# Scaling tokens by expert weights: one weight load in 1 KB runs with block transposes, a first tile in two pieces, and a 512-byte store by each DMA engine

## The chip, the cores and the metric

The kernel runs on one core of a Trainium2 chip. The metric is the device time of one execution in microseconds. Data lies in the chip's HBM; a kernel brings it into the on-chip memory (SBUF, 128 partitions) by DMA, computes there, and stores it by DMA. The core has 16 DMA engines, which serve the queues of all issuing engines. Two engines issue DMAs here: SyncE (SP), through the queue that the profile calls q1, and ScalarE (ACT), through q10. The two compute engines at work are VectorE (DVE) and ScalarE.

## The reference

```python
batch, seq, hidden, k = 16, 1024, 512, 2
x_expanded = x[:, :, np.newaxis, :].repeat(k, axis=2)
weights = expert_weights[..., np.newaxis]
return (x_expanded * weights).astype(np.float32)
```

Each of the 16384 tokens is a row of 512 float32 values. The output has two rows per token: the row times its first weight, and the row times its second. The expert indices are not used. The input is 33.6 MB, the output 67.1 MB, the weights 131 KB.

## The kernel before

The tokens are cut into eight groups of 2048. In a group, partition p holds 16 consecutive tokens (`TX = 16`), so that a group's input is one tile of 128 partitions by 8192 floats, 32 KB in one run for each partition (4 MB in all). `rows` (line 46) makes this view for input, output and weights alike. Input tiles come from `x_pool`, which has two buffers. A group is computed in two halves of eight tokens (`TO = 8`); each half fills one output tile of 128 by 8192 floats (4 MB) from `o_pool`, which has four buffers.

The weights are loaded first, by eight DMAs issued by SP (line 55), one for each group: 128 partitions by 32 floats, which is a run of 128 bytes for each partition. All end up in one tile `w_tile`, where column c of partition p is the weight that belongs to slot c of that partition's tokens.

`load(i)` (lines 69 to 77) takes an input buffer and issues the group's load from ScalarE (line 76). Two loads are issued ahead of the loop; after each group the load of the group after next follows. A load can be issued when both compute engines are through with the tile that had its buffer. In ScalarE's program it stands behind the first multiply of the next group.

The loop over a group's 16 tokens issues two multiplies for each: for `kk == 0` a `tensor_scalar` on VectorE (line 97), for `kk == 1` a `mul` on ScalarE (line 91). Each reads 512 columns of the input tile and one column of `w_tile`, and writes 512 columns of the output tile. After eight tokens SP issues the store of the output tile (line 105). SP and ScalarE work their programs in order: an instruction that waits holds up those behind it.

Of the kernel before, what the change touches and what calls it, by code (L numbers as in the profile page):

```python
# [1 line left out]

# [4 lines left out]


@with_exitstack
def kernel(  # L10
    ctx: ExitStack,
    tc: tile.TileContext,
    x: bass.AP,
    expert_indices: bass.AP,
    expert_weights: bass.AP,
    out: bass.AP,
):
    nc = tc.nc

    batch, seq, hidden = x.shape  # L20
    k = expert_weights.shape[-1]
    P = nc.NUM_PARTITIONS
    ntok = batch * seq
    assert ntok % P == 0
    A_TOTAL = ntok // P

    f32 = mybir.dt.float32
    row = k * hidden
    TX = 16
    TO = 8  # L30


    groups = [[16], [16], [16], [16], [16], [16], [16], [16]]
    assert sum(sum(g) for g in groups) == A_TOTAL

    xf = x.rearrange("b s h -> (b s) h")
    of = out.rearrange("b s k h -> (b s) (k h)")
    wf = expert_weights.rearrange("b s k -> (b s) k")

    w_pool = ctx.enter_context(tc.tile_pool(name="w_pool", bufs=1))  # L40
    x_pool = ctx.enter_context(tc.tile_pool(name="x_pool", bufs=2))
    o_pool = ctx.enter_context(tc.tile_pool(name="o_pool", bufs=4))

    w_tile = w_pool.tile([P, A_TOTAL * k], f32)

    def rows(of_all, done, T):
        return of_all[done * P : (done + T) * P, :].rearrange(
            "(p a) n -> p (a n)", a=T
        )

    weights = []
    for group in groups:
        weights.append((sum(n for _, n in weights), sum(group)))
    for at, T in weights:
        nc.sync.dma_start(out=w_tile[:, at * k : (at + T) * k], in_=rows(wf, at, T))

    tiles = []
    done = 0
    for group in groups:
        T = sum(group)  # L60
        a0 = 0
        for n in group:
            tiles.append((done, T, a0, n))
            a0 += n
        done += T

    loaded = []

    def load(i):
        if i >= len(tiles):  # L70
            return
        done, T, a0, n = tiles[i]
        x_tile = x_pool.tile([P, TX * hidden], f32)
        cols = rows(xf, done, T)[:, a0 * hidden : (a0 + n) * hidden]
        for lo, hi in [(0, P)]:
            nc.scalar.dma_start(out=x_tile[lo:hi, : n * hidden], in_=cols[lo:hi, :])  # L76
        loaded.append(x_tile)

    for i in range(2):
        load(i)  # L80
    for i, (done, T, a0, n) in enumerate(tiles):
        x_tile = loaded[i]
        outr = rows(of, done, T)
        for t in range(n):
            if t % TO == 0:
                o_tile = o_pool.tile([P, TO * row], f32)
            for kk in range(k):
                c = (done + a0 + t) * k + kk
                o = t % TO * row + kk * hidden
                if kk == 1:  # L90
                    nc.scalar.mul(  # L91
                        out=o_tile[:, o : o + hidden],
                        in_=x_tile[:, t * hidden : (t + 1) * hidden],
                        mul=w_tile[:, c : c + 1],
                    )
                    continue
                nc.vector.tensor_scalar(  # L97
                    out=o_tile[:, o : o + hidden],
                    in0=x_tile[:, t * hidden : (t + 1) * hidden],
                    scalar1=w_tile[:, c : c + 1],  # L100
                    scalar2=None,
                    op0=mybir.AluOpType.mult,
                )
            if (t + 1) % TO == 0:
                nc.sync.dma_start(
                    out=outr[:, (a0 + t + 1 - TO) * row : (a0 + t + 1) * row],
                    in_=o_tile,
                )
        load(i + 2)

# [1 line left out]
_INS = ['x', 'expert_indices', 'expert_weights']  # L112
_OUTS = [((16, 1024, 2, 512), 'float32')]


# [23 lines left out]
```

## Time and profile before

| | |
|---|---|
| median of 12 runs | 240.16 us (240.04 to 241.89) |
| the profiled execution | 240.13 us |
| its span, first to last instruction | 238.3 us |
| VectorE busy | 52.0 us, 128 multiplies of 483 ns |
| ScalarE busy | 81.4 us, 128 multiplies of 711 ns and a table load of 1.28 us |
| DMA packets on SP's queue | 3456, 67.24 MB |
| DMA packets on ScalarE's queue | 1152, 33.55 MB |
| HBM read, written | 33.69 MB, 67.11 MB |

The span is what the trace covers; 1.8 us of the measured time lie around it. A DMA is carried out as packets, one for each run of memory[...], with one packet of 4 bytes at the end that counts the DMA's semaphore. A large load or store is thus 128 packets of 32 KB, eight for each engine. The "DMA" row of the page gives the mean busy share of the 16 engines in tenths, for 40 slices of the span; the row "GB/s" gives what they moved, where the bytes of a packet count in the slice in which it starts. An instruction that issues a DMA ends long before the data lands: the landing has its own figure.

### The profile page before, as it was taken

What the parts mean: (1) busy time and instruction counts of PE and PEld (TensorE: products, weight loads), DVE (VectorE), ACT (ScalarE), POOL (GpSimd) and SP (SyncE); (2) the same over time, 40 slices, a digit from 0 to 9 for tenths busy, and PEclk for the clock granted to TensorE, in tenths of its full rate; (3) what the DMA queues carried; (4) which work ended last, traced back from release to release, by engine and by line L of the source; (5) the groups of instructions that cost most, each with busy time, mean ns of one, the idle gap of its engine ahead of it and who ended that gap; (6) DMA issues with size and microseconds to landing.
All of it is one profiled execution on the core that took longest, in us unless ns stands there. A gap on an engine that the chain in (4) does not pass through costs nothing.

```text
span 238.3 us, 384 instructions
## 1 busy us (share of the span) xinstructions
DVE 52.0 (22%) x128; ACT 81.4 (34%) x129; POOL 0.2 (0%) x4
## 2 busy tenths in 40 slices
DVE  0072900055005004050230503214040235000000
ACT  2078960076107007080260803417043256200000
POOL 0000000000000000000000000000000000000000
DMA  6999999999999999999999999999999999999996
GB/s 267 442 442 362 435 434 429 418 429 418 434 440 440 432 440 440 434 429 434 423 429 429 429 434 440 440 434 434 440 429 429 440 423 429 429 429 434 440 440 264
DMA packets 4610, 100.81 MB, mean 423 GB/s; under 512 B 1536, under 2 KB 1536, under 8 KB 1536
## 3 DMA queue, kind: packets, MB, share of 16 engines
q1 hardware_dynamic: 3456, 67.24, 65.6%
q10 hardware_dynamic: 1152, 33.55, 33.1%
q14 instruction: 2, 0.02, 0.0%
HBM read 33.69 MB, written 67.11 MB: 423 GB/s over the span
## 4 chain that ended last, share of the span: by engine, by line
DMA 60%; another core or an unknown queue 12%; ACT 12%; ACTq 1%; issue 0%
DMA out_dram<-o_tile 41%; DMA x_tile<-in_x_dram 18%; ACT o_tile L91 12%; DMA w_tile<-in_expert_weights_dram 1%; ACTq L76 0%; ACTq L134 0%; ACTq L91 0%
## 5 line engine op out<-in xcount | busy, mean ns | idle before, releaser
L91 ACT ACTIVATE o_tile<-x_tile,w_tile 128x512 f32<-128x512 f32 x128 | 80.2, 711 | 118.6 <-DMA out_dram<-o_tile 96.1
L97 DVE TENSOR_SCALAR o_tile<-x_tile,w_tile 128x512 f32<-128x512 f32 x128 | 52.0, 483 | 150.2 <-DMA out_dram<-o_tile 115.7
L91 ACT ACT_TABLE_LOAD x1 | 1.3, 1283 | 3.8 <-DMA w_tile<-in_expert_weights_dram 3.8
L123 POOL MEMSET const-bfloat16-1.0<- 128x1 bf16 x1 | 0.1, 103 | 0.0
L123 POOL MEMSET const-uint8-127<- 128x1 uint8 x1 | 0.1, 102 | 0.0
L123 POOL MEMSET const-float32-0.0<- 128x1 f32 x1 | 0.1, 100 | 0.2 <-issue 0.2
L123 POOL MEMSET const-float32-1.0<- 128x1 f32 x1 | 0.1, 99 | 0.0
## 6 DMA issues: line engine op xcount, KB each, us to landing
out_dram<-o_tile SPq DMA_DIRECT2D x16, 4096.0 KB, 48.3
x_tile<-in_x_dram ACTq DMA_DIRECT2D x8, 4096.0 KB, 23.2
w_tile<-in_expert_weights_dram SPq DMA_DIRECT2D x8, 16.0 KB, 21.1
```

The lines of the kernel that those rows point to most:

```text
L91: nc.scalar.mul(out=o_tile[:, o : o + hidden], in_=x_tile[:, t * hidden : (t + 1) * hidden], mul=w_tile[:, c : c + 1],)
L97: nc.vector.tensor_scalar(out=o_tile[:, o : o + hidden], in0=x_tile[:, t * hidden : (t + 1) * hidden], scalar1=w_tile[:, c : c + 1], scala ...
L123: nc = _bacc.Bacc("TRN2", target_bir_lowering=False, num_devices=1)
```

## The change

The eight weight loads become one DMA, issued by ScalarE ahead of all input: the weights are read as 128 runs of 256 floats (1 KB) into `w_in`. They then lie in the wrong partitions. One VectorE transpose of 128 by 256 turns each 32 by 32 block, into `w_mid`, and 16 transposes of 32 partitions by 64 elements move and turn the blocks into their places in `w_tile`. The layout of `w_tile` is that of before.

SP issues one additional store ahead of all else: a tile `early` of 16 partitions by 128 floats, which VectorE sets to zero, goes to the first 512 bytes of 16 output rows, 128 rows apart, one row for each DMA engine. The real stores write these rows later.

The first group's input is loaded by two DMAs, each of eight tokens for every partition (16 KB runs). ScalarE has one small multiply on the loaded weights (`unused`) ahead of the loop. The multiplies are given out by `c % 3`: every third goes to ScalarE, the others to VectorE (171 and 85, for 128 and 128). The number and size of the output tiles, the stores and the seven other input loads are as before.

```diff
-    weights = []
-    for group in groups:
-        weights.append((sum(n for _, n in weights), sum(group)))
-    for at, T in weights:
-        nc.sync.dma_start(out=w_tile[:, at * k : (at + T) * k], in_=rows(wf, at, T))
+    w_in = w_pool.tile([P, R * C], f32)
+    w_mid = w_pool.tile([P, R * C], f32)
+    w_tile = w_pool.tile([P, G * C], f32)
+    nc.scalar.dma_start(out=w_in, in_=wf.rearrange("(p n) -> p n", p=P))
+    early = w_pool.tile([16, 128], f32)
+    nc.vector.memset(early, 0.0)
+    nc.sync.dma_start(
+        out=of[: P * TX, :128].rearrange("(e t) n -> e t n", e=16)[:, 0, :], in_=early
+    )
...
-        for lo, hi in [(0, P)]:
-            nc.scalar.dma_start(out=x_tile[lo:hi, : n * hidden], in_=cols[lo:hi, :])
+        at = 0
+        for n in [8, 8] if i == 0 else [TX]:
+            cols = slice(at * hidden, (at + n) * hidden)
+            nc.scalar.dma_start(out=x_tile[:, cols], in_=rows(xf, i)[:, cols])
+            at += n
...
+    nc.vector.transpose(out=w_mid, in_=w_in)
+    GQ = G // (P // B)
+    for dst in range(P // B):
+        for src in range(P // B):
+            nc.vector.transpose(
+                out=w_tile[
+                    dst * B : (dst + 1) * B, src * GQ * C : (src + 1) * GQ * C
+                ],
+                in_=w_mid[src * B : (src + 1) * B, :].rearrange(
+                    "c (q g h j) -> c g h j q", q=R, g=GQ, h=P // B
+                )[:, :, dst],
+            )
+    unused = w_pool.tile([P, 1], f32)
+    nc.scalar.mul(out=unused, in_=w_in[:, :1], mul=w_in[:, :1])
...
-                c = (done + a0 + t) * k + kk
+                c = i * C + t * k + kk
...
-                if kk == 1:
+                if c % 3 == 2:
```

Here `P` is 128, `B` is 32, `TX` is 16, `k` is 2, `C` is 32, `R` and `G` are 8.

More of the change, by code (lines that the diff above doesn't have):

```diff
@@ L30 @@
     TO = 8
-    groups = [[16], [16], [16], [16], [16], [16], [16], [16]]
-    assert sum(sum(g) for g in groups) == A_TOTAL
+    G = A_TOTAL // TX
+    C = TX * k
+    B = 32
+    R = 8
+    assert A_TOTAL % TX == 0 and C == B and G * (P // B) == B and A_TOTAL * k == R * B
     xf = x.rearrange("b s h -> (b s) h")
     of = out.rearrange("b s k h -> (b s) (k h)")
-    wf = expert_weights.rearrange("b s k -> (b s) k")
+    wf = expert_weights.rearrange("b s k -> (b s k)")
     w_pool = ctx.enter_context(tc.tile_pool(name="w_pool", bufs=1))
@@ L42, with rows @@
     o_pool = ctx.enter_context(tc.tile_pool(name="o_pool", bufs=4))
[L44 to L48, printed above, removed]
-        )
-    weights = []
-    for group in groups:
-        weights.append((sum(n for _, n in weights), sum(group)))
-    for at, T in weights:
[L55 to L65, printed above, removed]
+    def rows(of_all, g):
+        return of_all[g * P * TX : (g + 1) * P * TX, :].rearrange(
+            "(p a) n -> p (a n)", a=TX
+        )
+    w_in = w_pool.tile([P, R * C], f32)
[7 more added lines that the diff above has]
+    )
     loaded = []
     def load(i):
-        if i >= len(tiles):
+        if i >= G:
             return
-        done, T, a0, n = tiles[i]
         x_tile = x_pool.tile([P, TX * hidden], f32)
-        cols = rows(xf, done, T)[:, a0 * hidden : (a0 + n) * hidden]
-        for lo, hi in [(0, P)]:
-            nc.scalar.dma_start(out=x_tile[lo:hi, : n * hidden], in_=cols[lo:hi, :])
+        at = 0
[3 more added lines that the diff above has]
+            at += n
         loaded.append(x_tile)
@@ L80 @@
         load(i)
-    for i, (done, T, a0, n) in enumerate(tiles):
+    nc.vector.transpose(out=w_mid, in_=w_in)
[12 more added lines that the diff above has]
+    nc.scalar.mul(out=unused, in_=w_in[:, :1], mul=w_in[:, :1])
+    for i in range(G):
         x_tile = loaded[i]
-        outr = rows(of, done, T)
-        for t in range(n):
+        for t in range(TX):
             if t % TO == 0:
@@ L95 @@
                     )
[L96 to L103, printed above, removed]
+                else:
+                    nc.vector.tensor_scalar(
+                        out=o_tile[:, o : o + hidden],
+                        in0=x_tile[:, t * hidden : (t + 1) * hidden],
+                        scalar1=w_tile[:, c : c + 1],
+                        scalar2=None,
+                        op0=mybir.AluOpType.mult,
+                    )
             if (t + 1) % TO == 0:
                 nc.sync.dma_start(
-                    out=outr[:, (a0 + t + 1 - TO) * row : (a0 + t + 1) * row],
+                    out=rows(of, i)[:, (t + 1 - TO) * row : (t + 1) * row],
                     in_=o_tile,
```

## The prediction

> **What bounds the kernel now.** I read the page's 40 slices first, then the span cut into stretches, then the single microseconds of the worst stretch, then the waits, and last the DMA packets. From the page:
>
> ```profile
> DMA  6999999999999999999999999999999999999996
> GB/s 267 442 442 362 435 434 429 418 429 418 434 440 440 432 440 440 434 429 434 423 429 429 429 434 440 440 434 434 440 429 429 440 423 429 429 429 434 440 440 264
> ...
> DMA packets 4610, 100.81 MB, mean 423 GB/s; under 512 B 1536, under 2 KB 1536, under 8 KB 1536
> ```
>
> The 16 DMA engines are busy from the first slice to the last, while VectorE has 52.0 us of work and ScalarE 81.4 us in 238.3. What is to be seen is where the rate falls below its level: in the first slice, the fourth and the last. The stretches give the sizes (columns: stretch and length, busy time of the engines, clock, DMA share, GB/s):
>
> ```profile
> 0.00:1.00 1.00, 0.00 (x0) 0.00 (x0) 0.20 (x4) 1.00 0.00 0
> 1.00:4.00 3.00, 0.00 (x0) 0.23 (x1) 0.00 (x0) 1.00 0.84 300
> 4.00:20.00 16.00, 6.43 (x16) 7.86 (x13) 0.00 (x0) 1.00 1.02 436
> 20.00:24.00 4.00, 0.13 (x1) 3.25 (x7) 0.00 (x0) 1.00 0.99 293
> 24.00:48.00 24.00, 6.87 (x18) 10.46 (x17) 0.00 (x0) 1.00 1.01 434
> 48.00:204.00 156.00, 38.53 (x95) 59.66 (x96) 0.00 (x0) 1.00 1.00 433
> 204.00:236.00 32.00, 0.00 (x0) 0.00 (x0) 0.00 (x0) 1.00 1.00 432
> 236.00:238.30 2.30, 0.00 (x0) 0.00 (x0) 0.00 (x0) 1.00 0.00 0
> ```
>
> Loads with stores (24 to 204) and stores alone (204 to 236) run at the same 432 to 434, so the middle and the end have nothing to give. 100.81 MB at 433 are 232.8 us. What is not streaming: 1.00 us before any packet; 3 x (1 - 300/433) = 0.92 in 1 to 4, where the first loads start up; 4 x (1 - 293/433) = 1.29 in 20 to 24; 2.3 at the end. Only the front can change. Inside the bad stretch (bytes count at a packet's start):
>
> ```profile
> 20.00:21.00 1.00, 0.00 (x0) 1.00 (x3) 0.00 (x0) 1.00 0.87 230
> 21.00:22.00 1.00, 0.00 (x0) 1.00 (x3) 0.00 (x0) 1.00 1.26 329
> 22.00:23.00 1.00, 0.00 (x0) 1.00 (x2) 0.00 (x0) 1.00 0.07 10
> 23.00:24.00 1.00, 0.13 (x1) 0.25 (x2) 0.00 (x0) 1.00 1.76 603
> ```
>
> The packet records say what happens. A 32 KB packet takes 1.213 us and follows the one before it on its engine after 1.209. The last 16 packets of the second load (from 20.7) take 1.81 to 2.37, mean 2.04: a **stall of 0.83 us** on every engine. Then 0.46 (1.29 - 0.83) goes until the first store's packets start at 23.3 to 23.9, and in it the engines work off a **backlog of weight packets**. The store had been issued at 18.24, but stood behind them on SP's queue:
>
> ```profile
> 0.73 12.79 SPq L55 DMA_DIRECT2D w_tile<-in_expert_weights_dram  x8
> 18.24 6.41 SPq L105 DMA_DIRECT2D out_dram<-o_tile  x2
> ...
> DMA to landing us min/median/max: 2.7/21.1/22.4
> ```
>
> The last line is for the weights: 16 KB take 21 us to land. The cause: from 6 to 20 us each engine takes one weight packet (13 ns) per 32 KB input packet.
>
> **A rule against the row.** The Trainium skill (DMA: Bandwidth & Descriptors, Queues, rings and completion order) has an engine drain a packet of 9 to 17 descriptors before it turns to the other queue. By that, the 64 weight descriptors of an engine would be through after some 5 input packets (64/13), no backlog would meet the store, and removing the weights would save only their own time. The records show one for one, so I go by the row: the backlog's 0.46 is real, and goes. By the rule my sum is 0.46 smaller.
>
> **The change part by part.**
>
> Weights: eight loads of 128 B runs (1024 packets) become one of 128 runs of 1 KB, ahead of the input on ScalarE's queue. Removed: the backlog, 0.46. Also the interleaving: an input packet with a weight packet before it starts 1.219 us after the last, not 1.209, for some 14 packets per engine: 0.14. Added at the front: 131 KB at 433 are 0.30, less the first weight load that stood there already (9 packets of about 11 ns, 0.10): +0.20. Issue order: the first input DMA is now second on ScalarE, and an issue there took 0.41. Bounds 0 to 0.41; before, the first input packets waited for a weight packet's end on each engine anyway (starts from 1.81 to 3.02), so I take 0.10.
>
> First tile in two pieces: 16 packets of 16 KB per engine for 8 of 32 KB, plus a semaphore packet, at some 10 ns each (the extra that a small packet cost above): bounds 0 to 0.10, taken 0.06. It brings the first computation forward. The first tile landed at 13.20; half its bytes are 4.84 us less, plus 0.36 for the additions: about 8.7. This is hidden, as is the next part.
>
> Transposes: 17 on VectorE, after the weights land (first weight load: 2.7 us after issue; here about 3.6). None is in the trace. The nearest row is the multiply of 512 elements, 483 ns, 396 start to start. Upper end: 16 x 0.40 + 0.48 = 6.9, done at 10.5. The Trainium skill (VectorE: DVE Perf Modes, The TRN2 errata) prices an SBUF operation at 58 cycles plus its elements: (58 + 64)/0.96 = 127 ns, so 16 x 0.127 + 0.33 = 2.4, done at 6.0. I take the middle, 8.3. Either way the first store can be issued between 13.1 and 14.9, against 18.24. The cover is the second load, whose packets last until about 22: between 6 and 8 us of slack (to 20.9, see the last rival).
>
> Split of the multiplies: every third one goes to ScalarE, so a half tile is 10 to 11 on VectorE (x 0.396 = 4.35) and 5 to 6 on ScalarE (x 0.612 = 3.4), against 5.01 for ScalarE's 8. Hidden behind 9.7 us of store per half tile; worth nothing. If compute set the pace, VectorE's 171 x 0.396 = 68 us in 238 would still be far from it.
>
> Small store: 16 x 512 B on SP, after a VectorE memset (about 0.1). Behind it on SP are only the real stores, the first due at 13; that one overwrites the same rows and so waits for this one's landing, long past. ScalarE's dummy multiply waits for the weights with only its table load and the multiplies behind it. Direct cost: a 512 B packet, about 0.03. **The unknown** is the 0.83 stall. It falls where each engine first has a store to this output ahead of it. If it is the price of a first store, the small store pays it at 2 to 3 us, when each engine's first packet is slow anyway (1.2 to 1.95 us). Bounds: it overlaps fully (0) or is added there (0.83). Taken 0.10, since both delays would be waits and not work.
>
> A second rule speaks against this part: the same DMA page gives each DMA a fixed cost of about 2.0 us (Anatomy of one DMA) and says to coalesce transfers under 64 KB (Rules for kernel authors). Read as time on the path, the 8 KB store and the extra piece are +4.0 and the time is over 242. The row: the first 16 KB weight load took 2.65 from issue to landing, yet input packets started from 1.81 on the same engines. It is latency beside other work; I do not charge it.
>
> Sum: -0.83 - 0.46 - 0.14 + 0.20 + 0.10 + 0.06 + 0.10 + 0.03 = -0.94. The profiled execution took 240.13 (span 238.3 and 1.8 around it), the median is 240.16, so nothing shifts between them: **239.2**.
>
> **Does anything starve later?** First store from about 14, alternating one for one with the second load: both end near 33. The second store (ready at 18) then has 9.7 us to run; the third load is issued when tile 1 arrives (33.5, behind ScalarE's first multiply of it, as before), and the third store is ready at about 38. SP's queue never empties, so from there it is the old steady state, paced by stores giving back buffers:
>
> ```profile
> DVE o_tile L97 <- DMA out_dram<-o_tile: 115.7, 11, 13.8
> ACT o_tile L91 <- DMA out_dram<-o_tile: 96.1, 11, 12.0
> ```
>
> Compute waits for stores, not stores for compute.
>
> **Rivals.**
>
> Stall stays: the 0.83 belongs to the first large store, or to any turn from loads to stores, or the small store adds it at the front. For it: the first 32 KB stores themselves are not slow, so the tie to a first store is a guess. Against: one for one at 6 to 20 us, reads of weights stalled nothing. Sum -0.94 + 0.83 = -0.1: 240.0. No measurable change.
>
> More is gained: ScalarE's weight load and the small store also absorb the slow start of the first input packets (0.6 at least of the 0.92 in 1 to 4): 239.2 - 0.7 = 238.5.
>
> Slower: the transposes bring the weights late. Reading with a stride, one might cost far more than the multiply. It decides when the first store is issued later than about 20.9, as the second load's packets end at 22 and an issue took 1.0 to its first packet. Less 4.35 of compute and 3.6 for the weights, 13.0 is left for 17: 0.76 us each. At 1 us each, 4 us more of idle DMA: 243.2. Against it: twice the longest VectorE instruction in the trace. The latency rule above would land on the same side.
>
> **Numbers.** Forecast 239.2: 0.56. More gained: 0.10. Stall stays: 0.25. Slower: 0.09. A measurement of this kernel tells 0.3% (0.7 us) from no change: faster is below 239.44, slower above 240.88. The forecast's own range is 238.7 to 239.7: issue order up to 0.31 dearer or 0.10 cheaper, a late disturbance of single engines (at 77.9 us two packets were 0.4 and 0.7 late) there or not, and a part of the first packets' slow start gained; about a tenth of it is past 239.44. Faster 0.62, same 0.29, slower 0.09. To hold 8 in 10 the range takes in both neighbours: 238.3 to 240.2.
>
> **What would show it.** Right: the fourth slice near 430; no packets over 1.3 us around the end of the second load; packets under 512 B near 430; first store issued between 13 and 15. The small store's part: first input packets not ending later than 4.4 us. Stall stays: packets near 2 us wherever the first large store begins. Wrong: idle DMA after 20 us, or a first store later than 20.9.

## The result

The changed kernel takes 241.83 us (median of 12 runs, 240.74 to 244.31), against 240.19 before (49 runs measured along with it, 240.01 to 242.05). The ratio is 1.0071, with a 95% interval of 1.0048 to 1.0093: slower by 1.6 us. The profiled execution took 241.28, with a span of 239.5, and is among the faster half of the 12; the one before took 240.13, with 238.3. The ratios here compare means and leave disturbed runs out (of these 12 the one of 244.31), so they need not equal the ratio of the two medians.

The page of the changed kernel, the row of busy DMA engines, the rate and the packets:

```profile
DMA  7999999999999999999999999999999999999995
GB/s 248 432 394 438 438 432 428 438 389 427 432 432 438 438 432 438 427 439 438 438 432 427 432 421 432 438 421 432 438 432 438 421 434 438 427 438 438 432 432 219
DMA packets 3779, 100.83 MB, mean 421 GB/s; under 512 B 432, under 2 KB 576, under 8 KB 576
```

The hole in the fourth slice (362 before) is gone, and the packets under 512 B went from 1536 to 432. These 432 are the 4-byte semaphore packets alone, one from each of the 16 engines for each of 27 DMAs; before, there were 512 of them and the 1024 of the weights. But there are new holes: 394 in the third slice and 389 in the ninth. In stretches of 3 us (columns as in the prediction: stretch, length, busy time of VectorE, ScalarE and GpSimd, clock, DMA share, GB/s):

```profile
12.00:15.00 3.00, 2.67 (x7) 1.55 (x3) 0.00 (x0) 1.00 1.02 437
15.00:18.00 3.00, 2.89 (x8) 1.63 (x3) 0.00 (x0) 1.00 1.04 350
18.00:21.00 3.00, 0.00 (x0) 0.00 (x0) 0.00 (x0) 1.00 1.12 470
46.00:49.00 3.00, 0.00 (x0) 0.00 (x0) 0.00 (x0) 1.00 1.14 492
49.00:52.00 3.00, 0.00 (x0) 0.00 (x0) 0.00 (x0) 1.00 0.98 350
```

The kernel before, two of the same stretches:

```profile
15.00:18.00 3.00, 3.00 (x9) 3.00 (x6) 0.00 (x0) 1.00 0.97 416
49.00:52.00 3.00, 1.69 (x5) 3.00 (x6) 0.00 (x0) 1.00 0.94 404
```

In both holes of the changed kernel the DMA engines are busy (shares of 1.04 and 0.98) while little is begun: their packets take longer. The packet records name them. From 15.0 to 18.4 it is the third to fifth packets of the second load, right after the first store was issued at 13.20. From 49.7 to 50.6 it is nearly always the seventh of the third load, 0.39 to 0.64 us late on each engine.

I followed the packets of each DMA engine (one starts where the one before it on that engine ended) and took the mean over the 16 engines. "Excess" is what a packet takes above the usual time of its size. 192 packets of 1.213 us, or as many bytes in smaller ones, are 232.9 us in both kernels. The rest:

| us, mean of the 16 engines | before | changed |
|---|---|---|
| start of the first input packet | 2.33 | 2.61 |
| excess of packets over their usual time, start to 8 us | 0.39 | 0.59 |
| the same, 8 to 26 us (first store) | 0.84 | 0.82 |
| the same, after 26 us | 0.11 | 0.80 |
| gaps less overlaps between packets, to 26 us | +0.54 | -0.08 |
| the same, after 26 us | -0.46 | -0.43 |
| mean end of an engine's work | 236.7 | 237.2 |
| end of the last engine's work | 237.20 | 238.13 |

The weights' backlog is gone, as predicted (0.54 to -0.08). The stall at the first store has stayed (0.84, 0.82). The start is 0.5 dearer. Read stalls, which are load packets that take longer than usual, have come in the middle of the run (0.80, against 0.11), where nothing was expected; some executions of the kernel before have them too, as a later section shows. And the last engine ends 0.9 after the mean, against 0.55: the time is that of the slowest engine, not of the mean. Of the 1.15 us between the two profiles 0.55 are the mean engine's, 0.4 the last engine's distance from it, and 0.2 come after the last packet.

### The profile page after: what moved, and what is told of

It is laid out like the page before. It is cut to its first block, busy times and chain, and to the rows that moved or that the text cites. A ratio compares the mean times of both kernels' runs of the same rounds, so it can differ in the third digit from the quotient of the medians.

```text
span 239.5 us, 397 instructions
## 1 busy us (share of the span) xinstructions
DVE 73.9 (31%) x189; ACT 55.2 (23%) x87; POOL 0.2 (0%) x4
## 4 chain that ended last, share of the span: by engine, by line
DMA 72%; DVE 7%; another core or an unknown queue 5%; ACTq 1%; issue 0%; DVEq 0%; ACT 0%; SPq 0%
DMA out_dram<-o_tile 40%; DMA x_tile<-in_x_dram 32%; DVE o_tile L118 7%; ACTq L79 0%; DVEq L155 0%; ACTq L60 0%; DVEq L118 0%; ACT o_tile L112 0%; SPq L126 0%; ACTq L112 0%
## 5 line engine op out<-in xcount | busy, mean ns | idle before, releaser
L118 DVE TENSOR_SCALAR o_tile<-x_tile,w_tile 128x512 f32<-128x512 f32 x171 | 68.9, 481 | 127.5 <-DMA out_dram<-o_tile 67.4
L112 ACT ACTIVATE o_tile<-x_tile,w_tile 128x512 f32<-128x512 f32 x85 | 53.7, 711 | 145.2 <-DMA out_dram<-o_tile 73.8
L90 DVE STREAM_TRANSPOSE w_tile<-w_mid 32x64 f32<-32x64 f32 x16 | 4.4, 276 | 0.3
```

The lines of the kernel that those rows point to most:

```text
L90: nc.vector.transpose(out=w_tile[dst * B : (dst + 1) * B, src * GQ * C : (src + 1) * GQ * C], in_=w_mid[src * B : (src + 1) * B, :].rearrange(
L112: nc.scalar.mul(out=o_tile[:, o : o + hidden], in_=x_tile[:, t * hidden : (t + 1) * hidden], mul=w_tile[:, c : c + 1],)
L118: nc.vector.tensor_scalar(out=o_tile[:, o : o + hidden], in0=x_tile[:, t * hidden : (t + 1) * hidden], scalar1=w_tile[:, c : c + 1], scala ...
```

## The experiments

Four theories were tried. **A**: the early first store costs, as it meets the second load in its middle. **B**: the small store costs. **D**: loads fall at other places among the stores later on, and stall. **F**: VectorE's additional instructions bring one more instruction fetch, which delays one DMA engine. **C** and **E** (the split's timing, and alignment) are told with their runs. Each kernel was timed against the kernel before, in turn on the same chip.

| kernel | median us (runs) | ratio to before, 95% interval |
|---|---|---|
| no_small_store | 242.10 (14) | 1.0066 [1.0042, 1.0089] |
| one_piece | 241.82 (12) | 1.0064 [1.0038, 1.0091] |
| even_split | 242.20 (7) | 1.0081 [1.0048, 1.0114] |
| weights_alone | 240.53 (22) | 1.0011 [0.9990, 1.0032] |
| weights_and_split | 241.64 (14) | 1.0055 [1.0036, 1.0074] |
| weights_and_pieces | 242.36 (6) | 1.0084 [1.0055, 1.0113] |
| weights_and_small_store | 241.08 (22) | 1.0023 [1.0007, 1.0039] |
| change_aligned | 241.90 (22) | 1.0039 [1.0022, 1.0056] |
| weights_aligned | 240.26 (22) | 0.9988 [0.9971, 1.0005] |
| before_shifted | 240.26 (22) | 0.9988 [0.9971, 1.0005] |
| before_more_dve | 242.12 (22) | 1.0056 [1.0040, 1.0071] |
| split_first_half | 241.17 (22) | 1.0036 [1.0016, 1.0056] |
| before_pieces | 240.53 (14) | 1.0014 [0.9993, 1.0036] |
| pieces_held | 241.22 (22) | 1.0031 [1.0012, 1.0050] |
| few_instructions | 243.17 (6) | 1.0112 [1.0083, 1.0140] |
| before_fewer_dve | 240.73 (22) | 1.0011 [0.9996, 1.0026] |
| more_dve_again | 242.27 (6) | 1.0083 [1.0064, 1.0102] |

### One part taken back at a time, and the weights alone

Without the small store:

```diff
-    early = w_pool.tile([16, 128], f32)
-    nc.vector.memset(early, 0.0)
-    nc.sync.dma_start(
-        out=of[: P * TX, :128].rearrange("(e t) n -> e t n", e=16)[:, 0, :], in_=early
-    )
```

> The changed kernel without the 512-byte store and its memset; all else as changed. Theory A (the early start of the large stores, inside the second load, is what costs: reads and stores are mixed from 14 us on): stays at 241 to 243, with the runs as far apart as with the change. Theory B (the small store costs): back to 239.2 to 240.2, runs within 0.5. Theory C (the uneven split of the multiplies costs, by shifting when stores are issued later on): stays at 241 to 243.

242.10: nothing comes back, and B falls as the sole cause. The trace also settles the unknown of the prediction, whether the small store takes over the stall of the first store. Without it, this kernel's stretch after the first store reads

```profile
15.00:18.00 3.00, 2.94 (x8) 1.66 (x3) 0.00 (x0) 1.00 1.04 350
```

and with it also 350 (above). The packets' excess there from 8 to 26 us is 0.78 on the mean engine without the small store and 0.82 with it. So the small store, though it is the first store to the output, neither causes the stall nor takes it away.

The first tile in one piece, and every second multiply on ScalarE:

```diff
-        for n in [8, 8] if i == 0 else [TX]:
+        for n in [TX]:
```

> The changed kernel with the first tile loaded by one DMA of 32 KB runs instead of two of 16 KB; all else as changed. The first store is then issued near 18, as before, with most of the second load done. Theory A (early start of the stores): 239.3 to 240.3 and runs within 1 us. Theory B (small store) and C (uneven split): stays at 241 to 243.

```diff
-                if c % 3 == 2:
+                if kk == 1:
```

> The changed kernel with every second multiply on ScalarE, as before, instead of every third; all else as changed. The first store is issued about 0.6 later than with the change. Theory C (the uneven split moves later stores): 239.3 to 240.3. Theories A (early stores) and B (small store): stays at 241 to 243.

Neither comes back (241.82, 242.20): no single part is the cause. All three taken back at once, which leaves the weights' part:

> Only the weights' part of the change, on the kernel before: one load of 1 KB runs ahead of the input, and the 17 transposes; no small store, first tile in one piece, even split. Theory A (early stores cost): first store near 18.5, the weights' backlog gone, 239.4 to 240.2. Theories B and C (the cost is in the small store or the split): 239.4 to 240.2 too. Above 240.9 would say that the weights' own change costs, which none of the three holds.

240.53, not to be told from before. So the weights' part does not cost, but it does not gain either. Its trace shows where its 0.6 went: the gaps to 26 us fell from 0.54 to -0.04, while the first input packets start 0.13 later, are 0.30 slower, and those at the first store 0.14 slower. This execution took 241.89 and has 0.89 of read stalls after 26 us. They are not a fixed price of the weights' part: the profiled execution of weights_aligned, the same kernel but for a wider tile (told below), took 240.01 and has 0.09.

### Each part added to the weights

The same three edits, one at a time in the other direction.

> The kernel with only the weights' part (240.5) plus the uneven split of the multiplies; no small store, first tile in one piece. Theory D (what costs are short read stalls after 26 us, 0.80 us per engine in the profile of the change against 0.11 before, and they come when loads fall at other places among the stores; the split moves the loads of the later tiles): 241 to 242.5. Theory B (small store) and A (early first store): 240.2 to 240.7.

> The weights' part plus the first tile in two pieces; no small store, even split. The first store is issued near 14, inside the second load. Theories A and D: 241 to 242.5, with read stalls after 26 us. Theory B: 240.2 to 240.7.

> The weights' part plus the 512-byte store; first tile in one piece, even split. Nothing but the start can move. Theory B (the small store costs): 241 to 242.5. Theories A and D: 240.2 to 240.8, like the weights alone.

The split costs 1.1 us (241.64 less 240.53) and the pieces 1.8, and their intervals do not overlap that of the weights alone. The small store costs 0.55 with intervals that overlap; 241.08 is above what A and D expected for it and within what B did, so that a part of B stays possible. Together the three cost 1.3 (241.83 less 240.53), not the sum: any two of them bring the time to about 242. That is what taking one back at a time had hidden.

The end of the trace with the split says how such a loss can look. Its execution of 242.89 is one of the two slowest of 14. The last microseconds of weights_and_split:

```profile
235.00:236.00 1.00, 0.00 (x0) 0.00 (x0) 0.00 (x0) 1.00 1.21 524
236.00:237.00 1.00, 0.00 (x0) 0.00 (x0) 0.00 (x0) 1.00 0.08 33
237.00:238.00 1.00, 0.00 (x0) 0.00 (x0) 0.00 (x0) 1.00 0.08 33
238.00:239.00 1.00, 0.00 (x0) 0.00 (x0) 0.00 (x0) 1.00 0.08 33
```

33 GB/s are one 32 KB packet in a microsecond. Fifteen engines end by 236.8; one works for three more packets, until 239.89. Followed back, this engine has a gap of 0.30 and a packet late by 0.36 at 30.8, the same again at 195.7, and packets late by 0.50 at 77.4 and by 1.11 at 160.7. In the gaps at 30.8 and 195.7 stand two packets of 8 KB, of 0.31 us each, on the queue that the page calls instruction. The page of the changed kernel has one more of them than the page before; first before, then changed:

```profile
q14 instruction: 2, 0.02, 0.0%
```

```profile
q14 instruction: 3, 0.02, 0.0%
```

In the changed kernel they come at 36.6, 105.9 and 195.1. The first and the last come when VectorE has begun its 57th and 198th instruction (all that its program runs, semaphore instructions included); the one between, at ScalarE's 68th, I take for ScalarE's. With 128 multiplies and 17 transposes VectorE has 171 such instructions in all (even_split), with 171 multiplies 214. That is theory F.

Seven traces have a second fetch of VectorE. In six of them (the changed kernel, no_small_store, change_aligned, weights_and_split and the two with 96 memsets, below) the DMA engine that carries it is the one that ends last, by 0.45 to 3.1 us; in one_piece it ends 0.15 before the last. In the changed kernel it ends at 238.13 and the next at 237.68, so the 0.65 of the second fetch can account for at most 0.45 of the 1.15 us between the two profiles. But the fetch is not needed for a slow kernel: even_split and weights_and_pieces have none, and took 242.20 and 242.36.

### Alignment of the big tiles

The dummy multiply's tile of one float moves all input and output tiles by 32 bytes, in the change and in every variant so far.

```diff
-    unused = w_pool.tile([P, 1], f32)
-    nc.scalar.mul(out=unused, in_=w_in[:, :1], mul=w_in[:, :1])
+    unused = w_pool.tile([P, 32], f32)
+    nc.scalar.mul(out=unused[:, :1], in_=w_in[:, :1], mul=w_in[:, :1])
```

> The changed kernel with the tile of the dummy multiply made 32 floats wide instead of one, all else the same. In the kernel before, input and output tiles begin in SBUF at bytes divisible by 128; in the change (and all variants so far) the one-float tile takes 32 bytes, so they begin at bytes divisible by 32 only (20128 against 17536). Theory E (alignment of the big tiles makes the DMA reads stall): 239.2 to 240.3. Theories A and D (early first store, places of the loads): stays at 241 to 243.

> The weights' part alone, with the dummy multiply's tile 32 floats wide, so that the big tiles begin at bytes divisible by 128. Theory E: 239.5 to 240.2, and the runs above 241 (7 of 22 with the one-float tile) mostly gone. Otherwise: as the weights alone, 240.5.

The other way about, on the kernel before:

```diff
     w_tile = w_pool.tile([P, A_TOTAL * k], f32)
+    pad = w_pool.tile([P, 1], f32)
+    nc.vector.memset(pad, 0.0)
```

> The kernel before, with a one-float tile (and one memset of it on VectorE, idle then) ahead of the input tiles, so that these begin 32 bytes later, at bytes divisible by 32 only. Theory E: 240.6 to 242, runs spread as with the change. Otherwise: 240.2, spread as before.

241.90, 240.26 and 240.26: the first is as slow as the change and the last as quick as before. (The second lies between the two expectations and decides nothing.) Theory E falls.

The profile of change_aligned also shows a typical execution, of 241.91 with a median of 241.90. Its mean engine ends at 236.84, only 0.2 after that of the kernel before; its last engine ends at 238.78, 1.6 after the last one before. That engine carries both fetches of VectorE (0.65 each), and it is 1.57 late at the first store, where the mean is 1.0, and 0.54 late at 161.3. Here nearly all of the loss is one engine's. (Two engines run in step at the end of this trace; that each must carry 184 packets of 32 KB tells them apart.)

### VectorE's second instruction fetch by itself

```diff
+    pad = w_pool.tile([P, 32], f32)
...
         load(i + 2)
+        for _ in range(24 if i < 4 else 0):
+            nc.vector.memset(pad, 0.0)
```

> The kernel before, with 96 small memsets on VectorE (some 0.1 us each, 74 of them before the first tile has arrived), so that VectorE runs through a second block of instructions and fetches once more. Theory F (each 8 KB instruction fetch delays one DMA engine by 0.65 us, VectorE's always the same one, and the slowest engine sets the end): 240.6 to 240.9. If fetches do not matter: 240.2.

> The kernel before with 96 memsets once more, for a profile of a typical execution: the one profiled took 241.09, while 18 of 22 took 241.88 to 242.37. Theory F: median near 242.1; in the profile the engine that VectorE's fetches delay ends last, by about 1.9 more than the others' usual spread of 0.9, with the fetches' delays in its packets. If it ends last for other reasons, the fetch is not the mechanism though it is the trigger.

And the control, 32 memsets:

```diff
+    pad = w_pool.tile([P, 32], f32)
+    for _ in range(32):
+        nc.vector.memset(pad, 0.0)
```

> Control for the 96 memsets: the kernel before with 32 of them, all ahead of the first tile. VectorE ends before its second instruction fetch. Theory F (it is the second fetch that cost 1.9 us): 240.2, as before. If memsets as such cost: 240.8 or more.

With 96 memsets 242.12 and 242.27, with 32 memsets 240.73 (1.0011, not to be told from before). The 96 cost 1.9 us in the median and 1.3 by the first ratio, more than theory F had given (240.6 to 240.9). A memset takes 85 ns on an engine that is idle for most of the run:

```profile
L112 DVE MEMSET pad<- x96: 85/85/85, 0.8 to 23.7; 128x32 f32 x96
```

In both traces with 96 the second fetch comes when VectorE has begun 198 instructions, exactly as in the changed kernel (at 137.0 and 138.2 us), and with 32 there is none. So the second fetch is the likeliest trigger. It is not the only difference, though: with 96 the first fetch comes at 11 to 12 us and not at 25, and the first store is issued at 18.8 to 19.0 and not at 18.3, though its packets begin at 23.2 to 23.3 in the control and in the second trace with 96 alike. The direct price shows in the first execution profiled, of 241.09. Its excess after 26 us is only 0.06 on the mean engine; its last engine has the fetch at 137.0 and a packet late by 0.35 at 137.4, 0.65 together, and ends at 238.16, where the next ends at 237.08 and the last of the kernel before at 237.20.

Most executions take a further microsecond, and the second trace shows it. From 84 to 88 us, first before_more_dve, then more_dve_again:

```profile
84.00:88.00 4.00, 0.00 (x0) 0.00 (x0) 0.00 (x0) 1.00 1.08 467
```

```profile
84.00:88.00 4.00, 0.00 (x0) 0.00 (x0) 0.00 (x0) 1.00 0.97 344
```

In the second, all 16 engines have a packet of the fifth load late, by 0.67 us on the mean. The engine with both fetches ends last, at 239.33, the next at 238.30. The last microseconds of more_dve_again (in the kernel before, nothing is begun after 236):

```profile
236.00:237.00 1.00, 0.00 (x0) 0.00 (x0) 0.00 (x0) 1.00 0.46 197
237.00:238.00 1.00, 0.00 (x0) 0.00 (x0) 0.00 (x0) 1.00 0.15 66
238.00:239.00 1.00, 0.00 (x0) 0.00 (x0) 0.00 (x0) 1.00 0.08 33
```

From 84 to 88 us the control's profile, of an execution of 241.29, has a hole too, and the kernel before, of 240.13, has none:

```profile
84.00:88.00 4.00, 0.00 (x0) 0.00 (x0) 0.00 (x0) 1.00 1.03 385
```

```profile
84.00:88.00 4.00, 0.00 (x0) 0.00 (x0) 0.00 (x0) 1.00 1.06 459
```

So the stall in the middle of the run is nothing that the change invented. Of the 49 executions of the kernel before, 35 took 240.01 to 240.43 and 14 took 241.09 to 242.05. Of the five profiles of kernels with its loads and stores, the three that took 241.29 (the control), 241.54 (before_shifted) and 242.26 have a read stall between 84 and 90 us, and the two that took 240.13 and 241.09 have none. With the 96 memsets the slower executions became more frequent (20 of 22 took 241.88 or more, and two 241.02 and 241.09). Why is open.

### Is it the fetch or the timing with the split?

```diff
-                if c % 3 == 2:
+                if (c % 3 == 2) if i < G // 2 else (kk == 1):
```

> The weights' part (aligned variant, 240.26) plus the uneven split, but only in the first four of eight groups; the others even. VectorE then runs some 22 instructions fewer than with the split everywhere and ends before its second 8 KB instruction fetch. Theory F (the split costs by that fetch): 240.2 to 240.7. Theory D (the split costs by moving loads and stores): 241.2 or more, like the split everywhere (241.6).

241.17, between the two: 0.9 above weights_aligned, 0.5 below the split everywhere. No second VectorE fetch came during the work (VectorE had 192 instructions). So the split costs without the fetch too, with half of it 0.9; the changed timing is what D would blame. Whether the other 0.5 is the fetch is not shown: half of the split is missing as well, and the two intervals overlap.

The other direction, no fetch at all, was tried on the kernel before with few and long instructions:

```diff
+            if i > 0 and t % TO == 0:
+                c = (done + a0 + t) * k
+                for kk in range(k):
+                    nc.vector.tensor_tensor(
+                        out=o_tile.rearrange("p (t k h) -> p t k h", k=k, h=hidden)[:, :, kk, :],
...
+                        op=mybir.AluOpType.mult,
+                    )
```

> The kernel before, but in the groups after the first VectorE does eight tokens with one multiply by a broadcast weight column (4096 elements, some 4.3 us), for both outputs, and ScalarE only issues loads: 28 instructions for 224, so that no engine comes to an instruction fetch in the run. Theory F: the two engines that the fetches delay (0.7 to 0.9 us each in the profile before) no longer end last: 239.4 to 240.0. If fetches do not set the end: 240.2 or more.

243.17, a miss. Not one 8 KB fetch is in the span, and yet it is the slowest of all. VectorE now needs 8.8 us for eight tokens:

```profile
L90 DVE TENSOR_TENSOR o_tile<-x_tile,w_tile 128x4096 f32<-128x4096 f32 x28 | 122.6, 4421 | 67.1 <-DMA out_dram<-o_tile 55.4
```

It still waits 55.4 us for stores, so it is not the bound; but all loads and stores came at other times, and packets after 26 us are late by 0.64. It changes too much to speak on F.

### Why the pieces cost

Two kernels keep the pieces and move the first store back. In the first, the weights' backlog holds it back (the kernel before, first load in two):

```diff
-        for lo, hi in [(0, P)]:
-            nc.scalar.dma_start(out=x_tile[lo:hi, : n * hidden], in_=cols[lo:hi, :])
+        for lo, hi in [(0, 8), (8, 16)] if i == 0 else [(0, TX)]:
+            part = slice(lo * hidden, hi * hidden)
+            nc.scalar.dma_start(out=x_tile[:, part], in_=cols[:, part])
```

> The kernel before with its first tile in two pieces and nothing else: eight weight loads on SP's queue. The first store can be issued near 14, but stands behind the weights' packets until the second load is through. Theory A (the pieces cost because the first store meets the second load in the middle): 239.9 to 240.5. If the pieces as such (16 KB packets, one more load) cost: 241 or more.

In the second, ScalarE waits for the second piece ahead of its first multiply:

```diff
+            if i == 0 and t == 0:
+                nc.scalar.mul(
+                    out=o_tile[:, hidden : hidden + 1],
+                    in_=x_tile[:, TX * hidden - 1 : TX * hidden],
+                    mul=w_tile[:, :1],
+                )
```

> The weights' part plus the first tile in two pieces (aligned), with one small ScalarE multiply that makes ScalarE wait for the second piece ahead of its first multiply, so that the first store is issued near 18.5 and not near 14. Theory A: 240.2 to 240.7, like the weights alone. If the pieces as such cost: 241.5 or more, like weights and pieces (242.4).

240.53 and 241.22, against 242.36 for weights and pieces. The issue of the first store in the three traces, weights_and_pieces, before_pieces and pieces_held:

```profile
13.73 192.56 SPq L121 DMA_DIRECT2D out_dram<-o_tile  x16
```

```profile
17.31 188.51 SPq L106 DMA_DIRECT2D out_dram<-o_tile  x16
```

```profile
19.50 185.87 SPq L127 DMA_DIRECT2D out_dram<-o_tile  x16
```

The first 32 KB store packets begin at 18.2, 21.8 and 22.9. The first result is at the upper edge of what A expects. The second lies between the two expectations: it takes back 1.1 of the 1.8 to 2.1, and stays 0.9 above weights_aligned with intervals that do not overlap. So the better part of the pieces' price goes with the early first store, and a part does not (the hold itself brings the store 1 us later than without pieces). In the trace of weights_and_pieces the stall at the first store is uneven: the engine that ends last was 1.62 late there in one packet (mean 0.8) and 1.39 late in a read stall at 66.4 (mean 0.38). It ends at 239.30, the mean at 236.9. These two packets make that engine the last one in this execution; that the same holds in others is not shown.

## Why the prediction was wrong

Forecast 239.2, range 238.3 to 240.2, faster; measured 241.83, slower. Two steps failed: the stall of 0.83 at the first store was to go and stayed, which takes the gain away; and "Only the front can change" left the price of the early first store and of the split at nothing, which put the sign wrong. The steps one by one:

- **The backlog and the interleaving, -0.60:** right in size. The gaps to 26 us fell by 0.62. The row that stood against the Trainium skill's rule of whole packets (DMA: Bandwidth & Descriptors, Queues, rings and completion order) was the right one to go by: one for one, the backlog was real.
- **The start, +0.36 and 0.13 for the small store:** about right; measured 0.28 for the first packet's start and 0.20 for its slowness, 0.48 in all. The small store's landing took 2.1 us on the page, near the 2 us of the second rule (the Trainium skill, DMA: Bandwidth & Descriptors, Anatomy of one DMA, states them for DMAs issued by GpSimd; this one is SyncE's), and nothing waited for it. That these 2 us were not charged was right, within what weights_and_small_store can tell (0.55, intervals overlapping).
- **The stall, -0.83:** this step failed. "If it is the price of a first store, the small store pays it": it does not. The excess stays at 0.82, and is 0.78 without the small store. The rival "stall stays" had this right. With it alone the time would have been 240.0.
- **The places and times of the front:** right. Transposes took 276 ns each, between the bounds of 127 (an estimate by the Trainium skill's formula, VectorE: DVE Perf Modes, The TRN2 errata) and 400 (by the row), near the 263 that the middle comes to; the first store was issued at 13.20, of 13.1 to 14.9 given:

```profile
3.44 4.63 DVE L90 STREAM_TRANSPOSE w_tile<-w_mid 32x64 f32<-32x64 f32 x16
...
13.20 5.11 SPq L126 DMA_DIRECT2D out_dram<-o_tile  x2
```

- **"Only the front can change", and the split "worth nothing":** this failed. I read the middle as having nothing to give, which was so, and took from it that it had nothing to lose. The split was costed by VectorE's time, which is hidden. That it moves loads and stores, and that 17 transposes and 43 multiplies more lead past VectorE's 198th instruction and so to another fetch through the DMA engines, was not counted; the prediction noted two late packets at 77.9 us as a disturbance, and in the trace two instruction fetches stand beside them, at 77.8 and 78.0. Measured: 1.1 us for the split added to the weights' part; of a fetch itself 0.65 on one engine, of which at most 0.45 tells in the profile of the change.
- **The early first store as a thing that is hidden:** failed too. It was costed at nothing, with 6 to 8 us of slack as a merit. The pieces that bring it cost 1.8 when added to the weights' part, and most of that is gone when the store is held back. Which of the two, pieces or split, costs more in the change itself is not shown: taking either back alone returns nothing.
- **The sum over a mean engine:** all terms were rates over 16 engines. The end is that of the slowest one. Its distance from the mean grew by 0.4 between the two profiles, and from 0.55 to 1.9 in the typical execution of change_aligned.
- The rival on the slower side put the price on late transposes. They were on time: the side was right, the mechanism was not.

What stays open: what sets off the read stalls in the middle of the run. They come in the kernel before as well, all engines at once, and kernels that differ only in their start or in idle-time memsets have them more or less often. That they follow from where loads meet stores was argued and not shown. Nor is it shown why the prices of the parts do not add up, although a maximum over engines would do that.

## What to carry to other kernels

Where all DMA engines are busy to the end, a change can lose in stretches that have nothing to gain: ask what it adds to their traffic at any time, instruction fetches among it, and look at when each engine ends, not at the mean rate. Instructions added to an idle engine need not be free: 32 small ones could not be told from none here, 96, with which the program reached one more fetch, cost 1.3 to 2.0 us. Bringing the first store forward was no merit here, where the loads ahead of it still filled the engines.

## What the runs showed of the hardware

- An instruction fetch of 8 KB held one DMA engine for 0.31 us and, in the changed kernel, made its next packet late by 0.35. In the seven traces with two fetches by VectorE they came at its 56th to 76th and then at its 197th or 198th instruction; in six of the seven, as far as an engine's packets can be followed, both fell on the same DMA engine.
- The stall when the first large store begins (0.75 to 1.2 us on the mean engine in all 19 profiles) falls on input packets already under way, not on the store's own, the first 128 of which take 1.213 to 1.222 us in the changed kernel. A small store ahead of it does not take it away.
- A load issued beside full queues had its first packet some 3.6 us later (31.57 to 35.2 in the changed kernel, 47.49 to 51.1 before), against about 1.0 at the start (the weights' load of the changed kernel, 0.72 to 1.75), when the engines were idle.
